# RWKV-7 recurrence stage: one step for both head pairs of a group, row-tiled image products, decay applied after the add, masks read from PSUM

## The chip, the cores and the metric

The kernel runs on one core of a Trainium2 chip. The metric is device time in microseconds (us) of one execution of the whole program. TensorE (PE) multiplies into PSUM, VectorE (DVE) and ScalarE (ACT) work element by element and can read PSUM, GpSimd (POOL) works element by element on SBUF alone, and SyncE (SP) issues most DMA transfers. Each engine runs its instructions in a fixed order and waits on semaphores for the others.

## The reference, cut to what matters

The program is two layers of a hybrid backbone over 1024 latent and 256 context tokens: an attention and RG-LRU layer, a mixture of experts, an RWKV-7 time-mixing layer, and a second mixture of experts. The change touches the RWKV-7 recurrence alone, which runs in both directions for 16 heads of 64 x 64 state:

```python
def wkv_scan(s0, decay, k, v, kk, a, r, reverse):
    ...
    def step(s, inp):
        w_t, k_t, v_t, a_t, b_t = inp[:5]
        sa = jnp.einsum('bhvk,bhk->bhv', s, a_t)
        s = s * w_t[:, :, None, :] + sa[..., None] * b_t[:, :, None, :] + v_t[..., None] * k_t[:, :, None, :]
        y = jnp.einsum('bhvk,bhk->bhv', s, inp[5]) if r is not None else None
        return s, y
    s_fin, ys = lax.scan(step, s0, xs, reverse=reverse)
    ...
```

It runs over the context first and then, from that state, over the latent tokens.

## The kernel before, in words

Class `Wkv` (lines 1880 to 2196) computes the recurrence in chunks of C = 64 tokens. There are 20 chunks (4 of context, 16 latent) for each of 4 head groups (`pg`), and so 80 group-chunks. A group holds two head pairs (`i`) in two directions (`d`): four units `u`, each with two heads `h` on the two halves of the partitions. Groups 0 and 1 go through all chunks together, then groups 2 and 3. Eight group-chunks (two groups, four chunks) make a batch, so there are ten batches.

- `prep` (L1937) handles two chunks of one group. It loads the key images `bk` and the query images `ar` by DMA. The product `G` (L1977) gives, for each unit, all products of the two within a chunk. In `ar` the two heads lie side by side with zeros in the other half (the memsets L1964 and L1965), so that one 128-row product serves both heads. ACT copies the solve's part of `G` into `lab` (L1981, L1982) and the output part into `lrb` (L1984); DVE multiplies the part for `ar` by a triangular mask (L1987) and POOL masks `lrb` in place (L1990). POOL scales the key images by the chunk's total decay `gC` into `bs` (L1956); PE transposes `bs` (L1996) and ACT copies it out as `bkt` (L1997). `G` has one buffer of two PSUM banks.
- `solve` (L2020) inverts the triangular matrices of one batch, all 32 units at once. It transposes `lab` into `lp` (L2028), runs 62 dependent DVE instructions of 31 to 256 elements (L2036, L2037), and transposes the result back (L2039 into `lp`, and four quarter transposes L2043 into `dtb`).
- `join` (L2046) completes the inverse: PE (L2055, which reads `lp`), ACT (L2058), PE (L2062), ACT (L2064). `lp`, `rp` and `tmp` have one buffer each, so the next solve can't start before the join has read `lp`.
- `values` (L2001) transposes the values into `sv`.
- `step` (L2066) advances one pair `i` of one group by one chunk. Its PE products are X (L2077), U (L2082), the first part of Y (L2087), S (L2093) and the second part of Y (L2101), with `xs` (L2079) and `sv` (L2089) copied by ACT between them. DVE adds the decayed state `pg` to S (L2116), ACT copies the sum into the next chunk's `sv` (L2120), and POOL multiplies the sum by `gC` for the step after (L2125). ACT copies Y out (L2129).

`run` (L2138) emits the work: `prep` up to 17 group-chunks ahead (as many buffers as `ar`, `lrb` and `bkt` have), `solve` and `join` of a batch just ahead of its steps. The order on each engine is then chosen by the framework's scheduler, from a simulated timeline with the emission order as priority, and is fixed in the program. In what follows a position is one group-chunk going through `step`.

After the recurrence, `mix_out1` multiplies the outputs by the output matrix and prepares the second mixture of experts; its pieces are named `tail` and are partly woven into the last steps.

Of the kernel before, what the change touches and what calls it, by code (L numbers as in the profile page):

```python
# [1879 lines left out]
class Wkv:  # L1880
# [20 lines left out]
    def __init__(self, g, p, pp):  # L1901
# [35 lines left out]
    def prep(self, b):  # L1937
# [16 lines left out]

        bs = self.bs.rearrange("p (c u x) -> p c u x", c=2, u=4)
        nc.gpsimd.tensor_tensor(bs, bk, g.gC[:, c0:c0 + 2, 4 * pg:4 * pg + 4, None].to_broadcast([128, 2, 4, 2 * C]), op=ALU.mult)  # L1956
        for k in range(2):
# [6 lines left out]
            nc.gpsimd.memset(ar[64:128, :, 0:w], 0.0)  # L1964
            nc.gpsimd.memset(ar[0:64, :, 2 * C:2 * C + w], 0.0)  # L1965
# [100 lines left out]
    def step(self, b, gr, i, nxt, ys, dense=False):  # L2066

        g, nc, p, pp = self.g, self.g.nc, self.p, self.pp
        ar, lrb, bkt, sv, c, dtb = gr["ar"], gr["lrb"], gr["bkt"], gr["sv"], gr["c"], b["dtb"]
# [3 lines left out]
        us = slice(2 * i, 2 * i + 2)
        X, U, S, Y = (ps[:, k] for k in range(4))
        for h, d in HD:
            u = 2 * i + d
            nc.tensor.matmul(X[R[h], C * d:C * d + C], ar[:, u, 2 * C * h:2 * C * h + C], sv[:, u, C * h:C * h + C], start=True, stop=True)  # L2077
        xs = p.tile([128, 2, C], F, name="xs", tag="xs", bufs=self.XB)
        nc.scalar.copy(xs, X.rearrange("p (d v) -> p d v", d=2))  # L2079
        for d in range(2):  # L2080
# [293 lines left out]
```

## Time and profile before

| quantity | value |
|---|---|
| median of 3 runs | 3741.8 us (3740.38 to 3742.62) |
| profiled execution | 3742.38 us, of which the span 3740.6 us |
| first image product to last output of the recurrence | 2220 us to 3012 us |
| the ten solves on DVE | first starts at 2239.9 us, last at 2839.7 us |
| mean granted clock of TensorE | 0.93 |
| busy share of the span | PE 88%, DVE 73%, ACT 62%, POOL 28% |

The profile is of one execution, taken by the hardware profiler. PE's busy time is that of its records, whose ends are modelled and include the time in which a result drains; a float32 matmul leaves two records. "Idle before" in a group of instructions is how long the engine stood still ahead of them, and the name behind the arrow is what ended that.

### The profile page before, as it was taken

The numbers are of one execution on the slowest core, as the hardware profiler recorded it, in microseconds if no ns is written. First come the engines' busy times: TensorE is split into PE (matmuls) and PEld (weight loads), VectorE is DVE, ScalarE is ACT, GpSimd is POOL, SyncE is SP. The second block draws the span as 40 slices with busy tenths as digits, with TensorE's granted clock in tenths as the row PEclk, the third lists the DMA queues.
The fourth block names the chain that finished last, engine by engine and source line by source line (L and its number), as shares of the span: only waits on it lengthen the run. The fifth ranks groups of instructions, "written<-read, shape, count | busy, mean of one in ns | idle before, by whom it ended". The sixth has DMA issues, their size and how long they took to land. (4 is left out here: it accounts for less than half of the span.)

```text
span 3740.6 us, 65805 instructions
## 1 busy us (share of the span) xinstructions
PE 3296.5 (88%) x25097; PEld 2565.2 (69%) x25097; DVE 2724.6 (73%) x3869; ACT 2312.7 (62%) x4629; POOL 1048.8 (28%) x1045
## 2 busy tenths in 40 slices
PE   7997989599999999697798867899897885999998
PEld 5884677477777777577776855677676564887776
DVE  5666773667666666667976987778678557888888
ACT  4564573366666666335644654788787554778776
POOL 2213002211111111235734663444344222111111
PEclk9998999799999999898898986999898897999999
DMA  5217715478888887335753773333335569999995
GB/s 199 64 31 278 271 56 182 158 265 283 294 286 281 280 296 275 112 116 159 223 148 92 213 193 80 88 92 96 85 92 156 162 207 330 380 379 385 354 381 217
DMA packets 579363, 770.45 MB, mean 206 GB/s; under 512 B 106868, under 2 KB 371048, under 8 KB 572904
## 3 DMA queue, kind: packets, MB, share of 16 engines
q1 hardware_dynamic: 564104, 717.22, 57.6%
q0 software_dynamic: 14944, 49.03, 4.8%
q8 instruction: 198, 3.24, 0.4%
q14 instruction: 117, 0.96, 0.1%
HBM read 638.96 MB, written 127.18 MB: 205 GB/s over the span
## 5 line engine op out<-in xcount | busy, mean ns | idle before, releaser
L192 DVE TENSOR_TENSOR elo<-raw,ehi 128x2048 fp32r<-128x2048 f32 x378 | 859.6, 2289 | 296.0 <-ACT ehi L191 294.8
L191 ACT ACTIVATE ehi<-raw 128x2048 fp32r<-128x2048 f32 x384 | 734.8, 1917 | 212.1 <-PE h L1158 82.6
L1158 PE MATMUL h<-ehi,xhi 128*128 128x512 f32 x512 | 208.0, 406 | 0.0
L1158 PE MATMUL h<-elo,xhi 128*128 128x512 f32 x512 | 202.9, 396 | 0.0
L1158 PE MATMUL h<-ehi,xlo 128*128 128x512 f32 x512 | 202.8, 396 | 0.0
L1102 PE MATMUL h<-ehi,wx 128*128 128x512 f32 x512 | 163.3, 396 | 0.0
L1477 PE MATMUL pj<-mvh,whi 128*128 128x384 f32 (+1 forms) x512 | 149.8, 326 | 2.9 <-ACT vv L1787 2.9
L1477 PE MATMUL pj<-mvl,whi 128*128 128x256 f32 (+1 forms) x512 | 147.3, 322 | 3.8 <-POOL mvl L192 2.9
L1477 PE MATMUL pj<-mvh,wlo 128*128 128x256 f32 (+1 forms) x512 | 149.1, 323 | 0.9 <-POOL wlo L192 0.7
L2037 DVE TENSOR_TENSOR rp<-rp,tmp 128x31 f32<-128x31 f32 (+15 forms) x310 | 141.8, 457 | 8.2
L1977 PE MATMUL G<-ar,early 128*128 128x256 f32 (+1 forms) x440 | 127.2, 443 | 22.2 <-issue 9.9
L1265 PE MATMUL y<-ehi,wh 128*128 128x512 f32 x512 | 143.6, 397 | 1.9 <-DVE wh L192 1.9
L1122 POOL DMA_INDIRECT xg<-s_hl,idx x16 | 15.8, 985 | 451.2 <-PE tr L1137 446.8
L2036 DVE TENSOR_TENSOR tmp<-lp,rp 128x31 f32<-128x31 f32 (+15 forms) x310 | 127.4, 411 | 8.1
L1080 ACT ACTIVATE xm<-tr,c_mcol 128x128 f32<-128x128 f32 x256 | 95.3, 452 | 60.9 <-PE tr L1069 35.9
L2120 ACT COPY sv<-st 64x128 f32<-64x128 f32 x304 | 89.9, 296 | 59.7 <-DVE st L2116 54.8
L1087 POOL DMA_INDIRECT xg<-s_hl,idx x16 | 24.1, 1509 | 361.4 <-PE tr L1069 339.1
L191 ACT ACTIVATE whi<-wraw 128x1024 fp32r<-128x1024 f32 x62 | 65.5, 1057 | 88.3 <-PE pj L1477 54.9
L1977 PEld LDWEIGHTS G<-ar,early 128*128 128x128 f32 x440 | 91.6, 232 | 41.0 <-issue 17.8
L216 PE MATMUL pj<-xhi,whi 128*128 128x512 f32 (+1 forms) x336 | 119.1, 355 | 0.0
L216 PE MATMUL pj<-xlo,whi 128*128 128x512 f32 (+1 forms) x336 | 119.0, 354 | 0.0
L216 PE MATMUL pj<-xhi,wlo 128*128 128x512 f32 (+1 forms) x336 | 118.8, 354 | 0.0
(565 smaller groups left out, 9772.7 us busy)
## 6 DMA issues: line engine op xcount, KB each, us to landing
raw<-in_exp_w SPq DMA_DIRECT2D x379, 1024.0 KB
modw<-in_mod_w SPq DMA_DIRECT2D x48, 1024.0 KB
wraw<-in_rw_rkv SPq DMA_DIRECT2D x48, 512.0 KB
s_iAR<-ar SPq DMA_DIRECT2D x32, 384.0 KB
s_iBK<-bk SPq DMA_DIRECT2D x32, 384.0 KB
ar<-s_iAR SPq DMA_DIRECT2D x88, 128.0 KB
early<-s_iBK SPq DMA_DIRECT2D x40, 256.0 KB
early<-s_iBK SPq DMA_DIRECT2D x80, 128.0 KB
```

What stands on the lines that cost most here:

```text
L191: nc.scalar.activation(hi, src, AF.Copy)
L192: (sub or nc.vector).tensor_tensor(lo, src, hi.bitcast(F), op=ALU.subtract)
L216: nc.tensor.matmul(ps[:m, :b - a], wt[:, k, :m], xt[:, k, a:b], start=k == 0 and n == 0, stop=k == kt - 1 and n == 2)
L1080: self.nc.scalar.activation(f[:, k], src[:, k], AF.Identity, scale=a, bias=b)
L1102: nc.tensor.matmul(hs[which], a[:, kk], b[:, k], start=kk == 0 and a is x[0] and b is w[1], stop=kk == 7 and a is x[1])
L1158: nc.tensor.matmul(hs[which], a[:, kk], b[:, k], start=kk == 0 and a is x[0] and b is w[1], stop=kk == 7 and a is x[1])
L1265: nc.tensor.matmul(y[:, 512 * n:512 * n + 512], a[:, kk % 4], b[:, k, 512 * n:512 * n + 512], start=kk == 0 and a is hh and b is hi, stop= ...
L1477: nc.tensor.matmul(ps[q], wk[:, k], xk[:, a:b], start=k == 0 and n == 0, stop=k == KT - 1 and n == 2)
L1977: nc.tensor.matmul(gp[:, u, :, 0:w], bk[:, k, u], ar[:, u].rearrange("p (h x) -> p h x", h=2)[:, :, 0:w], start=True, stop=True)
L2036: nc.vector.tensor_tensor(t, lp[:, k + 1:, k:k + 1].to_broadcast([128, n, w]), rp[:, k:k + 1, 0:w].to_broadcast([128, n, w]), op=ALU.mult)
L2037: nc.vector.tensor_tensor(rp[:, k + 1:, 0:w], rp[:, k + 1:, 0:w], t, op=ALU.subtract)
L2120: nc.scalar.copy(nxt(R[h], C * h), st[R[h]])
```

## The change

- `step` takes both pairs of a group at once. Each of its five products has eight matmuls of the four units in a row (heads alternating), each ACT copy and DVE instruction is of twice the width, and there is half their number. X and U lie in one PSUM bank, S and Y in a second; `XS` has two buffers of two banks where it had four of one. The first part of Y is emitted ahead of U.
- The product `G` is split by heads: each unit has two matmuls over 64 rows (row tiles at partitions 0 and 64) that write to two different banks, in place of one over 128 rows with zeros. The memsets of `ar` go.
- The decay is applied to the sum: DVE adds the old state to S and then multiplies the sum by `gC`. POOL's scaling of `bk` into `bs` and POOL's product `pg` go; the transposes read `bk`.
- DVE writes the masked `lrb` straight from PSUM; ACT's copies and POOL's mask of `lrb` go.
- In `solve`, one transposition over all partitions and two ACT copies take the place of four quarter transpositions into `dtb`.

```diff
-    NX = 4
+    NX = 2
...
-        bs = self.bs.rearrange("p (c u x) -> p c u x", c=2, u=4)
-        nc.gpsimd.tensor_tensor(bs, bk, g.gC[:, c0:c0 + 2, 4 * pg:4 * pg + 4, None].to_broadcast([128, 2, 4, 2 * C]), op=ALU.mult)
...
-            nc.gpsimd.memset(ar[64:128, :, 0:w], 0.0)
-            nc.gpsimd.memset(ar[0:64, :, 2 * C:2 * C + w], 0.0)
...
-            gp = pp.tile([128, 4, 2, gw], F, name="G", tag=gt, bufs=bufs)
+            gp = pp.tile([128, 2, 4, 2 * C], F, name="G", tag=gt, bufs=bufs)
...
-                nc.tensor.matmul(gp[:, u, :, 0:w], bk[:, k, u], ar[:, u].rearrange("p (h x) -> p h x", h=2)[:, :, 0:w], start=True, stop=True)
+                for h, own, oth, cc in HH:
+                    nc.tensor.matmul(gp[:, h, u, 0:w], bk[own, k, u], ar[own, u, cc:cc + w], start=True, stop=True)
...
-                if not ctxt:
-                    nc.scalar.copy(lrb[own], gp[own, :, h, C:])
...
-                nc.vector.tensor_tensor(o4, g4, self.mask[oth, None, :, 0:w].to_broadcast([64, 2, 2, w]), op=ALU.mult)
-            if not ctxt:
-                lb = lrb.rearrange("p (i d) t -> p i d t", d=2)
-                nc.gpsimd.tensor_tensor(lb, lb, self.mask[:, None, :, C:].to_broadcast([128, 2, 2, C]), op=ALU.mult)
+                parts = [(ar[oth, :, cc:cc + w], oth, slice(0, w))] + ([] if ctxt else [(lrb[own], own, slice(C, 2 * C))])
+                for out, r, x in parts:
+                    o4, g4 = (t.rearrange("p (i d) t -> p i d t", d=2) for t in (out, gp[r, h, :, x]))
+                    nc.vector.tensor_tensor(o4, g4, self.mask[r, None, :, x].to_broadcast([64, 2, 2, x.stop - x.start]), op=ALU.mult)
...
-                nc.tensor.transpose(tp[:, u], bs[:, k, u], g.ident)
+                nc.tensor.transpose(tp[:, u], bk[:, k, u], g.ident)
...
-        for q in range(4):
-            r = slice(32 * q, 32 * q + 32)
-            o = 32 * (q % 2)
-            nc.vector.transpose(dtb[r, :, o:o + 32].rearrange("p u t -> p t u"), rp[r])
+        nc.vector.transpose(dtb[:, :, 32:].rearrange("p u t -> p t u"), rp)
+        for h in range(2):
+            a = slice(64 * h, 64 * h + 32)
+            nc.scalar.copy(dtb[a, :, 0:32], dtb[a, :, 32:])
...
+        for h, u in HU:
+            nc.tensor.matmul(X[R[h], u], ar[:, u, 2 * C * h:2 * C * h + C], sv[:, u, V[h]], start=True, stop=True)
+        xs = p.tile([128, 4, C], F, name="xs", tag="xs", bufs=self.XB)
+        nc.scalar.copy(xs, X)
...
+            st = p.tile([128, 4, C], F, name="st", tag="st", bufs=3)
+            if c:
+                nc.vector.tensor_tensor(st, S, self.st.pop(pg), op=ALU.add)
+            gc = g.gC[:, c, 4 * pg:4 * pg + 4, None]
+            nc.vector.tensor_tensor(st, st if c else S, gc.to_broadcast([128, 4, C]), op=ALU.mult)
             for h in range(2):
+                nc.scalar.copy(nxt[R[h], :, V[h]], st[R[h]])
+            self.st[pg] = st
```

Line numbers shift by the lines removed: L1969 is the new G product, L1979 the new masks, L2017 and L2029 the first and last transposition of a solve, L2025 and L2026 its 62 instructions, L2086 the add and L2088 the product by `gC`, and on ACT L1973 and L1974 `lab`, L1986 `bkt`, L2003 and L2004 `sv` from `values`, L2067 `xs`, L2075 `sv` from U, L2090 the next `sv`, L2095 Y.

On DVE, from the end of the fifth solve to the start of the sixth (a batch of context chunks), the order before is:

```order
L2043 STREAM_TRANSPOSE dtb_19741<-rp 32x32x32 x4
L2116 TENSOR_TENSOR st<-XS,pg 128x128
L1987 TENSOR_TENSOR ar<-G,wmask 64x4x64 x2
L2116 TENSOR_TENSOR st<-XS,pg 128x128 x3
L1987 TENSOR_TENSOR ar<-G,wmask 64x4x64 x2
L2028 STREAM_TRANSPOSE lp<-lab 128x1024
```

The changed kernel has there, as the first twelve of its rows:

```order
L2029 STREAM_TRANSPOSE dtb_19741<-rp 128x32x32
L1979 TENSOR_TENSOR ar<-G,wmask 64x4x64 x2
L2086 TENSOR_TENSOR st<-XS,st 128x256
L2088 TENSOR_TENSOR st<-st,gC 128x256
L1979 TENSOR_TENSOR ar<-G,wmask 64x4x64 x2
L2086 TENSOR_TENSOR st<-XS,st 128x256
L2088 TENSOR_TENSOR st<-st,gC 128x256
L2086 TENSOR_TENSOR st<-XS,st 128x256
L2088 TENSOR_TENSOR st<-st,gC 128x256
L1979 TENSOR_TENSOR ar<-G,wmask 64x4x64 x4
L2086 TENSOR_TENSOR st<-XS,st 128x256
L2088 TENSOR_TENSOR st<-st,gC 128x256
```

Between two solves there stood the masks of two group-chunks and the adds of two positions; now there stand the masks of six group-chunks and the adds of six positions, and correspondingly fewer inside the solves. Over the solves 2 to 9 the counts inside a solve go from 94 `ar` masks and 92 adds of one pair to 42 `ar` masks, 38 `lrb` masks and 42 instructions of the new add and product; after a solve they go from 34 `ar` masks to 86 (5.4 group-chunks a gap).

On ACT, in steady state, a position with the copies of a `G` stands before as (two pairs' copies, `values`, and the first half of a `G`):

```order
L2120 COPY sv<-st 64x2x64 x2
L2129 COPY ys<-XS 128x2x64
L2014 COPY sv<-T 64x4x64
L2015 COPY sv<-T 64x4x64
L2120 COPY sv<-st 64x2x64 x2
L2129 COPY ys<-XS 128x2x64
L2120 COPY sv<-st 64x2x64 x2
L2129 COPY ys<-XS 128x2x64
L1981 COPY lab<-G 32x256
L1982 COPY lab<-G 32x4x32
L1984 COPY lrb<-G 64x256
```

and in the changed kernel as

```order
L2075 COPY sv<-XS 64x4x64 x2
L1986 COPY bkt<-T 128x512
L2067 COPY xs<-XS 128x256
L2003 COPY sv<-T 64x4x64
L2004 COPY sv<-T 64x4x64
L2095 COPY ys<-XS 128x2x128
L2090 COPY sv<-st 64x4x64 x2
L1973 COPY lab<-G 32x256
L1974 COPY lab<-G 32x4x32
```

One copy over both pairs stands where two narrower ones stood, and no `lrb` copy follows those of `lab`.

## Rows read from the trace of the kernel before

**Rows 1.** Busy time of each engine in a window, whole recurrence: window, length, engines, clock, DMA.
```profile
2310.00:3012.00 702.00, 615.49 (x9230) 471.94 (x9230) 523.81 (x1033) 524.07 (x1826) 282.26 (x408) 0.91 0.43 114
```
**Rows 2.** Instructions of line 2028, the first transposition of each solve.
```profile
L2028 DVE STREAM_TRANSPOSE lp<-lab x10: 1911/1956/1978, 2239.9 to 2839.7; 128x1024 f32<-128x1024 f32 x10
```
**Rows 3.** Windows: the seven solves from 2379.8 us, the first and the sum.
```profile
2379.80:2433.20 53.40, 49.38 (x738) 39.04 (x734) 47.11 (x91) 42.82 (x139) 24.59 (x36) 0.97 0.44 104
...
sum 368.10, PE 327.30 PEld 262.62 DVE 331.38 ACT 298.33 POOL 164.41; mean PE 46.76 PEld 37.52 DVE 47.34 ACT 42.62 POOL 23.49
```
**Rows 4.** Windows: the seven gaps behind those solves, the sum.
```profile
sum 91.80, PE 83.38 PEld 68.03 DVE 27.21 ACT 70.77 POOL 28.76; mean PE 11.91 PEld 9.72 DVE 3.89 ACT 10.11 POOL 4.11
```
**Rows 5.** DVE by lines, 2379.8 to 2839.7 us: busy, mean ns, idle before, releasers.
```profile
L2037 DVE TENSOR_TENSOR rp<-rp,tmp 128x31 f32<-128x31 f32 (+15 forms) x217 | 99.8, 460 | 5.9
L2036 DVE TENSOR_TENSOR tmp<-lp,rp 128x31 f32<-128x31 f32 (+15 forms) x217 | 87.0, 401 | 5.6
L2043 DVE STREAM_TRANSPOSE dtb<-rp 32x1024 f32<-32x1024 f32 x28 | 53.7, 1919 | 0.3
L1987 DVE TENSOR_TENSOR ar<-G,wmask 64x512 f32<-64x512 f32 (+1 forms) x82 | 52.2, 637 | 27.3 <-ACT lrb L1984 19.6 <-ACT lab L1982 6.3
L2116 DVE TENSOR_TENSOR st<-XS,pg 128x128 f32<-128x128 f32 x104 | 28.5, 283 | 17.0 <-PE XS L2101 8.7 <-ACT sv L2120 3.0 <-PE XS L2093 2.5
L1987 DVE TENSOR_TENSOR early<-G,wmask 64x512 f32<-64x512 f32 x30 | 20.7, 688 | 24.6 <-ACT lrb L1984 24.1
L2039 DVE STREAM_TRANSPOSE lp<-rp 128x1024 f32<-128x1024 f32 x7 | 14.7, 2105 | 0.2
L2028 DVE STREAM_TRANSPOSE lp<-lab 128x1024 f32<-128x1024 f32 x7 | 13.7, 1957 | 23.8 <-ACT lab L1982 23.8
```
**Rows 6.** Timeline of DVE and POOL: start, length, engine, line, tiles.
```profile
2644.88 0.19 DVE L2036 TENSOR_TENSOR tmp<-lp,rp 128x31 f32<-128x31 f32 x1
...
2648.74 1.90 POOL L1956 TENSOR_TENSOR early<-early,gC 128x1024 f32<-128x1024 f32 x1
2648.81 2.00 DVE L2036 TENSOR_TENSOR tmp<-lp,rp 128x156 f32<-128x156 f32 x1
...
2667.74 0.43 DVE L2036 TENSOR_TENSOR tmp<-lp,rp 128x256 f32<-128x256 f32 x1
```
**Rows 7.** ACT by lines and shapes, 2379.8 to 2839.7 us.
```profile
L2120 ACT COPY sv<-st 64x128 f32<-64x128 f32 x213 | 63.1, 296 | 38.5 <-DVE st L2116 34.9
L2089 ACT COPY sv<-XS 64x128 f32<-64x128 f32 x224 | 58.2, 260 | 5.1 <-PE XS L2087 1.7 <-PE XS L2082 0.3
...
L1984 ACT COPY lrb<-G 64x256 f32<-64x256 f32 x97 | 35.5, 366 | 1.2
L1997 ACT COPY bkt<-T 128x512 f32<-128x512 f32 x56 | 32.9, 588 | 1.8 <-PE XS L2093 0.9
...
L2079 ACT COPY xs<-XS 128x128 f32<-128x128 f32 x110 | 26.3, 271 | 1.4
L2129 ACT COPY ys<-XS 128x128 f32<-128x128 f32 x94 | 25.0, 265 | 1.8
```
**Rows 8.** Timeline of PE: products of a step (x8 is four matmuls) and of G.
```profile
2496.57 0.46 PE L2093 MATMUL XS<-sv,bkt 128*64 128x64 f32 x8
...
2496.96 0.45 PE L2101 MATMUL XS<-sv,lrb 64*64 64x64 f32 x8
...
2507.77 1.20 PE L2077 MATMUL XS<-sv,ar 128*64 128x64 f32 x32
...
2508.95 1.97 PE L1977 MATMUL G<-ar,early 128*128 128x256 f32 x8
```
**Rows 9.** Line 1987 by shapes, 2219 to 3012 us: its narrow form.
```profile
L1987 DVE TENSOR_TENSOR ar<-G,wmask 64x256 f32<-64x256 f32 x22 | 9.3, 422 | 8.0 <-ACT lab L1982 6.3 <-issue 1.3
```
**Rows 10.** Timeline of DVE: start of the second solve, end of the last.
```profile
2309.30 1.95 DVE L2028 STREAM_TRANSPOSE lp<-lab 128x1024 f32<-128x1024 f32 x1 [5.04 <-ACT lab L1982]
...
2898.53 7.68 DVE L2043 STREAM_TRANSPOSE dtb<-rp 32x1024 f32<-32x1024 f32 x4
```

More of the change, by code (lines that the diff above doesn't have):

```diff
@@ L2064, in join, with step @@
                 nc.scalar.copy(dtb[a, u0:u0 + 16, 32:], tp[a])
-    def step(self, b, gr, i, nxt, ys, dense=False):
+    def step(self, b, gr, nxt, ys):
         g, nc, p, pp = self.g, self.g.nc, self.p, self.pp
-        ar, lrb, bkt, sv, c, dtb = gr["ar"], gr["lrb"], gr["bkt"], gr["sv"], gr["c"], b["dtb"]
-        ps = pp.tile([128, 4, 2 * C], F, name="XS", tag="XS", bufs=self.NX)
-        HD = [(h, d) for h in range(2) for d in range(2)]
+        ar, lrb, bkt, sv, pg, c, dtb = gr["ar"], gr["lrb"], gr["bkt"], gr["sv"], gr["pg"], gr["c"], b["dtb"]
+        ps = pp.tile([128, 2, 2, 4, C], F, name="XS", tag="XS", bufs=self.NX)
+        HU = [(h, u) for u in range(4) for h in range(2)]
@@ L2072, in step @@
         R = [slice(0, 64), slice(64, 128)]
[L2073 to L2080, printed above, removed]
-            for h in range(2):
-                nc.tensor.matmul(U[R[h], C * d:C * d + C], dtb[R[h], gr["lu"] + 2 * i + d], xs[R[h], d], start=True, stop=True)
@@ new lines, in step @@
+        V = [slice(C * h, C * h + C) for h in range(2)]
+        X, U, S, Y = ps[:, 0, 0], ps[:, 0, 1], ps[:, 1, 0], ps[:, 1, 1]
+        for h, u in HU:
+            nc.tensor.matmul(X[R[h], u], ar[:, u, 2 * C * h:2 * C * h + C], sv[:, u, V[h]], start=True, stop=True)
+        xs = p.tile([128, 4, C], F, name="xs", tag="xs", bufs=self.XB)
+        nc.scalar.copy(xs, X)
+        if ys is not None:
+            for h, u in HU:
+                nc.tensor.matmul(Y[R[h], u], ar[:, u, 2 * C * h + C:2 * C * h + 2 * C], sv[:, u, V[h]], start=u == 0, stop=False)
@@ new lines, in step @@
+        for h, u in HU:
+            nc.tensor.matmul(U[R[h], u], dtb[R[h], gr["lu"] + u], xs[R[h], u], start=True, stop=True)
+        for h in range(2):
+            nc.scalar.copy(sv[R[h], :, V[h]], U[R[h]])
+        if nxt is not None:
+            for h, u in HU:
+                nc.tensor.matmul(S[R[h], u], bkt[:, u, V[h]], sv[:, u, V[h]], start=ys is None, stop=ys is None)
+        if ys is not None:
+            for h, u in HU:
+                nc.tensor.matmul(Y[R[h], u], lrb[R[h], u], sv[R[h], u, V[h]], start=False, stop=u == 3)
@@ L2128, in step @@
             to = (slice(0, 4, 3), slice(2, 0, -1))[c % 2]
-            nc.scalar.copy(ys[:, to, i], Y.rearrange("p (d v) -> p d v", d=2))
+            nc.scalar.copy(ys[:, to], Y.rearrange("p (i d) v -> p d i v", d=2))
     def finish(self, pg, ys, n):
@@ L2190, in run @@
                 to = [x for bb in (b, bs.get(k + 1)) if bb for x in bb["gr"] if (x["pg"], x["c"]) == (pg, c + 1)][0]["sv"]
-            for i in range(2):
-                us = slice(2 * i, 2 * i + 2)
-                self.step(b, gr, i, to and (lambda r, o, us=us: to[r, us, o:o + C]), ys[pg] if c >= 4 else None, at >= self.DENSE)
+            self.step(b, gr, to, ys[pg] if c >= 4 else None)
             if c >= 4 and c % 2:
@@ L2255, in __init__ @@
         T = [pp.tile([128, 512], F, name="T", tag="T", bufs=w.NT) for _ in range(w.NT)]
-        X = [pp.tile([128, 512], F, name="XS", tag="XS", bufs=w.NX) for _ in range(w.NX)]
+        X = [pp.tile([128, 2, 512], F, name="XS", tag="XS", bufs=w.NX) for _ in range(w.NX)]
+        X = [t[:, k] for t in X for k in range(2)]
         self.n = {"y": 0, "b": 0}
```

55 lines of the change are left out of this document (6 added, 49 removed).

## The prediction

> **What bounds the kernel now.** I read the windows of the whole stage first. From the first step to the last output it takes 702 us, with PE busy for 615, ACT and DVE for 524 each and POOL for 282 [rows 1]. No engine is full, so the pattern of the stage counts. The instructions of the solve's first transposition show it: there are ten, the first at 2239.9 us and the last at 2839.7 us [rows 2], and the second at 2309.3 [rows 10]. From the second to the tenth that is 530.4 us, a cycle of 66.3 us for each batch of eight positions.
>
> Seven cycles cut into the solve itself (368.1 us, 52.6 each) and the gap behind it (91.8 us, 13.1 each) tell two different stories. Inside a solve DVE works 331.4 of 368.1 us [rows 3]; with the small pauses between 62 dependent instructions it is full, and the solve lasts as long as the sum of what DVE has in its order there. In a gap DVE works only 27.2 of 91.8 us, while PE is busy for 83.4 and ACT for 70.8 [rows 4]: there steps, join and the last products `G` of the next batch go through PE and ACT, and the next solve waits for `lab` from ACT (23.8 us of idle time on the row of L2028 [rows 5]). So a cycle is DVE's sum in the solve plus the rate of PE and ACT in the gap. Over both, PE has 410.7 us of 459.9 for 56 positions, 7.3 us each, and ACT 369.1, 6.6 each. The gap holds the adds of two positions and the masks of 2.1 group-chunks on average; 2.1 positions at 6.6 us are 13.8, which agrees with 13.1.
>
> **The solve's own instructions.** The 434 instructions of L2036 and L2037 took 186.8 us in seven solves, 26.7 each [rows 5]. Some were held up: one of 156 elements took 2.00 us beside a POOL product of 1.90 us that started just before it, where clean ones take 0.19 us at 31 elements and 0.43 at 256 [rows 6]. A line through those two (0.157 us plus 1.07 ns per element) over the 62 instructions, with 2 x 5456 elements (31 x 1 + 30 x 2 + ... + 1 x 31, twice), gives 21.4 us, so 5.3 us of each solve are such stalls. The change leaves POOL nothing but a few memsets there, so I take all of them away; the bounds are none and all.
>
> The Trainium skill (SBUF — State Buffer, Who interferes with whom) says that a VectorE instruction with two SBUF inputs fully blocks against a GpSimd instruction that reads SBUF, and one that only writes doesn't matter; by that rule the remaining memsets cost nothing and the new product by `gC` meets nobody. That changes the lower bound of this term only: none left would be right.
>
> The four quarter transpositions took 53.7 us for seven solves, 7.7 each; one over all partitions should take what L2039 takes, 2.1 us. With the other two (13.7 and 14.7 over seven, 4.1 each solve) the solve's own work falls from 38.4 us to 21.4 + 4.1 + 2.1 = 27.6, and the pauses of 11.5 us over seven stay, 1.6 each [rows 5].
>
> **What else DVE has inside a solve.** The new order puts 42 `ar` masks, 38 `lrb` masks and 42 adds or products into eight solves. An `ar` mask takes 0.69 us [rows 5], an `lrb` mask of half the width 0.42 [rows 9]. An add from PSUM over 256 columns doesn't exist before; it lies between 0.28 (the 128-column one [rows 5]) and 0.56 (twice that), and the 256-element instruction from SBUF at 0.43 and the 256-column mask from PSUM at 0.42 are nearest, so I take 0.42, for the product too. Together (29.0 + 16.0 + 17.6) / 8 = 7.8 us. The solve becomes 27.6 + 1.6 + 7.8 = 37.0 us, 15.6 less than now. That much is gained inside the solve, and the gap has to take what was moved out.
>
> **The gap.** It now holds the masks of 5.4 group-chunks, and so some five positions with their `G`. On ACT the step's copies are 172.6 us of the seven cycles; at double width the same work takes 0.403 us for the copy from SBUF (0.296 plus 0.107 for 128 more columns, the difference of 0.366 and 0.260) and 0.37 for those from PSUM, half as many, 121.9 us in all. The `lrb` copies (35.5) go, and 14 new copies in the solve come, about 1.0 us each by extending 0.588 at 512 columns [rows 7]. ACT falls to 297.5 us, 5.3 a position. On PE a group of four matmuls starts 0.39 us before the next; sixteen in a row take 1.20 us where four take 0.46, so a matmul costs 0.062 and the change of product 0.14. Ten groups of four become five of eight: 3.9 to 3.2 us. If the row tiles of `G` run two at a time, its 1.97 us halve [rows 8]. PE falls from 7.3 to about 5.7 us a position. DVE has 86 `ar` masks, 74 `lrb` masks and 78 adds or products in eight gaps, 15 us each. POOL's waits are off all of these paths and go at no price.
>
> At PE's or ACT's rate 5.4 positions take 29 to 31 us. Against that stands that PE and ACT have only some three positions to do in the 37 us of the solve and can run ahead there: the first adds and masks of the gap are ready when it opens. The copies that ACT's order holds between the end of a solve and the last `lab` copy of the next batch come to 22 us on average, at these durations, the floor. I take 25.5, in the middle; bounds 22 and 31. The cycle is then 62.5 us against 66.3, 3.8 less, over eight cycles 30 us. DVE's whole sum is 37 + 15 = 52 us, so it is at 84% and the next thing late.
>
> The Trainium skill (TensorEngine Tiling (Array Packing), PSUM Bottleneck) warns that tiling speeds up TensorE and not the evacuation of PSUM. No run shows it here yet. `G` keeps its one buffer, so by that rule the halved `G` would bring nothing in the gap, and the time would be that of the row tile rival below.
>
> **Ends of the stage.** The first cycle lasts 69.4 us (2239.9 to 2309.3). There solve and masks sum to 27.6 + 1.6 + 12 x 1.11 = 42.5 and the waits for `G` of the first batches remain, 10 us less (6 to 15). The last solve runs from 2839.7 to 2906.2 us [rows 2, 10] with pieces of the tail between; its own work falls by 10.8 us, and I take 9 (5 to 12). The eight steps behind it run among the tail's large matmuls, which don't change: 0 (10 faster to 5 slower). From 3012 us on nothing is touched; the second mixture of experts just starts earlier.
>
> **The sum.** 30 + 10 + 9 = 49 us off the profiled 3742.4 (which is 0.6 above the median of the runs): 3693 us. With a gap of 22 and the better ends: 7.3 x 8 + 15 + 12 + 10 = 95, 3647 us. With 31 and the worse ends: a cycle of 68, 14 lost, 11 won, 5 lost, 3750 us.
>
> **The rivals.**
> - *ACT and PE set the whole gap.* No running ahead: 29 us, a cycle of 66, nothing won in the cycles; the ends keep 19 us: 3723 us. For it speaks that the gap of before follows the rate so closely.
> - *The row tiles of G don't overlap.* What the trace shows to overlap are tiles in different columns (pairs of 64-column tiles in a step), never two row tiles over the same columns. Then 8 half-row matmuls take as long as `G` now, PE needs 6.6 us a position, the gap becomes 25.5 + 5.4 x 0.9 = 30.4 and the cycle 67.4: 9 lost in the cycles, 19 won, 3732 us.
> - *Recurrence latency (slower).* A position's add, product, two wide copies and the next X are now one chain, with two chains under way instead of four, and one more DVE instruction between S and `sv`, queued behind the solve. Its pieces sum to five products at 0.46, 0.37 of `xs`, two copies at 0.37, add and product 0.84, two copies at 0.40, some 4.5 us without queues, and two chains share a round. It decides once a round (two positions) is over 66.3 / 4 = 16.6 us. At 18 us the cycle is 72: 46 lost, 10 won, 3778 us. Against it: before, positions passed in steady state at 8.2 us each and DVE, the queue in question, lets an add through after one or two solve instructions.
> - *More is won.* Steps run ahead inside the solve as far as buffers go, and the gap is at its floor: 3647 us.
>
> **Chances.** Forecast 0.45, more won 0.15, gap at the rate 0.15, row tiles in series 0.12, latency 0.13. The range of 3640 to 3750 leaves out the latency case and little else. Faster by over 0.2% (7.5 us, about what a measurement of this kernel can tell from no change), under 3734: the forecast, the gain, the rate case and half of the row tile case, less what of the forecast lies beyond, 0.76; within 0.2% 0.11; slower 0.13.
>
> **What would show it.** The first transposition L2017 of the second to tenth solve should be 62 us apart (now 66.3), from L2017 to the end of L2029 37 us; the solve's instructions should sum to about 21.4 us with none near 2 us; the new add and product at 0.42 each; a `G` of 16 records at about 1.1 us, else the row tiles run in series. Wrong would be: solves of 45 us or more (DVE waits inside for late steps), gaps of over 31 us, or L2090 waiting for L2088 by tens of us in total beyond the 34.9 us for L2116 now.

## The result and the profile after

The changed kernel takes 3757.6 us (median of five runs, 3753.0 to 3766.7) against 3740.4 us (3728.0 to 3742.6) for the kernel before: a ratio of 1.0056, 95% interval 1.0033 to 1.0078. It is slower by 0.6%; the forecast was 3693 us, in a range of 3640 to 3750. The profiled execution, the longest of the five, took 3766.7 us, of which the span is 3764.9, 24.3 more than before.

Busy time in the recurrence, as in [rows 1] (window, length, PE, PEld, DVE, ACT, POOL, granted clock, DMA share, GB/s); the last Y copy starts at 3032.0 us where it started at 3012.0:

```profile
2310.00:3030.00 720.00, 576.89 (x9662) 458.07 (x9659) 485.70 (x1079) 434.69 (x1258) 54.49 (x49) 0.84 0.41 110
```

Every engine works less than in [rows 1] (PE 577 against 615, ACT 435 against 524, POOL 54 against 282), and the stage still takes longer. The first transposition of the solves, as in [rows 2]:

```profile
L2017 DVE STREAM_TRANSPOSE lp<-lab x10: 1924/1931/1949, 2243.0 to 2859.2; 128x1024 f32<-128x1024 f32 x10
```

The second starts at 2293.4, so eight cycles take 565.8 us, 70.7 each, where they took 66.3. Windows of the seven solves from 2360.1 us, and of the seven gaps behind them, the sums, as in [rows 3, 4]:

```profile
sum 254.80, PE 199.35 PEld 164.13 DVE 235.42 ACT 134.06 POOL 0.00; mean PE 28.48 PEld 23.45 DVE 33.63 ACT 19.15 POOL 0.00
...
sum 244.30, PE 193.13 PEld 166.62 DVE 109.08 ACT 173.78 POOL 16.97; mean PE 27.59 PEld 23.80 DVE 15.58 ACT 24.83 POOL 2.42
```

A solve lasts 36.4 us (before 52.6) and a gap 34.9 (before 13.1). Inside a solve PE now works 28.5 and ACT 19.2 of 36.4 us; before they worked 46.8 and 42.6 of 52.6. The new idle time of ACT and PE lies beside the solve. DVE by lines from 2360.1 to 2859.2 us, as in [rows 5]:

```profile
L2026 DVE TENSOR_TENSOR rp<-rp,tmp 128x31 f32<-128x31 f32 (+15 forms) x217 | 74.3, 343 | 6.8
L2025 DVE TENSOR_TENSOR tmp<-lp,rp 128x31 f32<-128x31 f32 (+15 forms) x217 | 74.2, 342 | 7.1
L1979 DVE TENSOR_TENSOR ar<-G,wmask 64x512 f32<-64x512 f32 (+1 forms) x82 | 51.8, 632 | 67.5 <-ACT lab L1974 58.5 <-PE T L1985 4.8 <-DMA ar<-s_iAR 3.5
L1979 DVE TENSOR_TENSOR lrb<-G,wmask 64x256 f32<-64x256 f32 x96 | 40.5, 422 | 1.6
L2088 DVE TENSOR_TENSOR st<-st,gC 128x256 f32<-128x256 f32 x52 | 23.0, 442 | 1.1
L2086 DVE TENSOR_TENSOR st<-XS,st 128x256 f32<-128x256 f32 x52 | 21.9, 422 | 21.5 <-PE XS L2081 18.5 <-ACT bkt L1986 1.5 <-PE XS L2078 0.5
L1979 DVE TENSOR_TENSOR early<-G,wmask 64x512 f32<-64x512 f32 x30 | 20.5, 683 | 43.5 <-ACT lab L1974 43.5
```

DVE now waits for ACT: 58.5 and 43.5 us ahead of its two groups of `ar` masks. ACT by lines in the same stretch, as in [rows 7], waits in its turn:

```profile
L2090 ACT COPY sv<-st 64x256 f32<-64x256 f32 x108 | 43.6, 403 | 14.6 <-DVE st L2088 12.0
...
L2095 ACT COPY ys<-XS 128x256 f32<-128x256 f32 x48 | 17.9, 372 | 59.2 <-DVE st L2086 58.8
```

The span's 24.3 us, from the starts and ends of the solves: the first solve starts 3.1 later, the first cycle is 19.0 shorter (50.4 against 69.4), eight cycles are 35.4 longer, the last solve is 12.3 shorter, its end to the last Y copy 12.8 longer (118.6 against 105.8), and the rest 4.3 longer.

### The profile page after: what moved, and what is told of

Its sections match the earlier page's. It is cut to its first block, busy times and chain, and to the rows that moved or that the text cites. A ratio compares the mean times of both kernels' runs of the same rounds, so it can differ in the third digit from the quotient of the medians.

```text
span 3764.9 us, 65798 instructions
## 1 busy us (share of the span) xinstructions
PE 3264.1 (87%) x25737; PEld 2560.1 (68%) x25737; DVE 2685.2 (71%) x3963; ACT 2228.6 (59%) x4065; POOL 783.8 (21%) x637
## 5 line engine op out<-in xcount | busy, mean ns | idle before, releaser
L1969 PE MATMUL G<-ar,early 64*128 64x128 f32 (+1 forms) x880 | 98.6, 361 | 76.2 <-DVE lrb L1979 50.4
L1969 PEld LDWEIGHTS G<-ar,early 64*128 64x128 f32 x880 | 83.1, 255 | 85.3 <-issue 44.2
L2019 POOL MEMSET rp<- 128x1024 f32 x10 | 9.5, 952 | 589.8 <-DVE dtb L2029 587.5
L1979 DVE TENSOR_TENSOR ar<-G,wmask 64x512 f32<-64x512 f32 (+1 forms) x110 | 69.4, 631 | 82.3 <-ACT lab L1974 73.0
L1165 PE MATMUL hc<-raw,xc 128*32 128x256 f32 x2048 | 117.1, 381 | 0.0
L191 ACT ACTIVATE whi<-wraw 128x1024 fp32r<-128x1024 f32 x62 | 65.5, 1056 | 84.4 <-PE pj L1477 51.7
L2025 DVE TENSOR_TENSOR tmp<-lp,rp 128x31 f32<-128x31 f32 (+15 forms) x310 | 108.0, 349 | 9.9
L2026 DVE TENSOR_TENSOR rp<-rp,tmp 128x31 f32<-128x31 f32 (+15 forms) x310 | 107.0, 345 | 9.5
```

Of the source, the lines that this page charges most:

```text
L191: nc.scalar.activation(hi, src, AF.Copy)
L1165: nc.tensor.matmul(hc[32 * q:32 * q + 32, :256], xcs[e][:, kk], raws[kk // 4, q // 2][:, kk % 4, 256 * (q % 2):256 * (q % 2) + 256], start ...
L1969: nc.tensor.matmul(gp[:, h, u, 0:w], bk[own, k, u], ar[own, u, cc:cc + w], start=True, stop=True)
L2025: nc.vector.tensor_tensor(t, lp[:, k + 1:, k:k + 1].to_broadcast([128, n, w]), rp[:, k:k + 1, 0:w].to_broadcast([128, n, w]), op=ALU.mult)
L2026: nc.vector.tensor_tensor(rp[:, k + 1:, 0:w], rp[:, k + 1:, 0:w], t, op=ALU.subtract)
```

## The experiments

Four theories were tested. Theory 1: the one buffer of `G` makes product, `lab` copies and masks a chain. Theory 2: the recurrence's latency sets the gap. The clock theory: with the row tiles of `G` the granted clock falls, and all products get slower. The order theory: the scheduler deals the row-tiled `G` another order on each engine, and that order costs. In the table, cycle is the mean from the second to the tenth solve's start, solve and gap the means of the eight in it, and clock is the granted clock there. The column "adds" counts the positions whose add stands inside a solve in DVE's order, a mean of eight; the first chunk of a group has no add and is left out (84 adds of one pair in the eight solves before, where the 92 above hold eight copies too). The kernel before took 3739.1 to 3740.9 us in these comparisons.

| kernel | us | ratio, 95% interval | cycle | solve | gap | clock | adds |
|---|---|---|---|---|---|---|---|
| before | 3740.4 | 1 | 66.3 | 53.2 | 13.1 | 0.92 | 5.25 |
| after | 3757.6 | 1.0056 (1.0033–1.0078) | 70.7 | 36.7 | 34.0 | 0.82 | 2.25 |
| g_split | 3765.8 | 1.006 (1.004–1.0079) | 72.9 | 42.9 | 30.0 | 0.77 | 3.5 |
| pairs_apart | 3765.5 | 1.006 (1.004–1.008) | 73.5 | 39.6 | 33.9 | 0.76 | 3.4 |
| lrb_undone | 3777.9 | 1.0093 (1.0076–1.011) | 73.1 | 35.3 | 37.8 | 0.79 | 2.25 |
| decay_undone | 3768.9 | 1.0076 (1.0053–1.0098) | 70.1 | 40.9 | 29.1 | 0.83 | 2.75 |
| g_rows_alone | 3818.2 | 1.021 (1.019–1.023) | 79.0 | 42.7 | 36.2 | 0.78 | 2.3 |
| g_wide | 3704.5 | 0.9898 (0.9881–0.9914) | 63.7 | 46.5 | 17.3 | 0.92 | 5.25 |
| g_twice | 3836.0 | 1.025 (1.0231–1.027) | 77.1 | 34.6 | 42.5 | 0.84 | 1.75 |
| g_wide8 | 3697.9 | 0.9888 (0.9872–0.9905) | 62.7 | 46.0 | 16.6 | 0.93 | 5.25 |
| rows_order_wide | 3683.4 | 0.9846 (0.9826–0.9865) | 60.9 | 45.3 | 15.6 | 0.87 | 5.25 |
| wide8_order_rows | 3809.8 | 1.0189 (1.0172–1.0206) | 73.8 | 37.6 | 36.2 | 0.88 | 2.25 |
| rows_dve_order | 3732.0 | 0.9984 (0.9974–0.9995) | 67.7 | 50.7 | 17.0 | 0.82 | 5.25 |
| rows_pe_act_order | 3749.7 | 1.0025 (1.0016–1.0035) | 70.0 | 37.0 | 33.0 | 0.79 | 2.6 |
| solve_alone | 3765.8 | 1.0071 (1.0054–1.0088) | 68.6 | 42.5 | 26.1 | 0.91 | 4.1 |
| solve_order_before | 3757.4 | 1.0037 (1.002–1.0055) | 67.2 | 48.2 | 18.9 | 0.90 | 5.2 |

### The two first theories of the gap

**g_split** gives each head of `G` a tile of its own:

```diff
-            gp = pp.tile([128, 2, 4, 2 * C], F, name="G", tag=gt, bufs=bufs)
...
+                gp = [pp.tile([128, 4, 2 * C], F, name=f"G{h}", tag=f"G{h}", bufs=1) for h in range(2)]
...
```

> The changed kernel with G as two PSUM tiles of one bank, one for each head, in place of one tile of two banks; nothing else. Theory 1 (the one G tile is a chain: product 1.16 us, lab copies 1.25, masks 2.25, and waits, one group-chunk every 5.8 us in the gaps): the two heads overlap, a group-chunk needs 4 us or less, the gap falls from 34.0 to about 26 us, the cycle from 70.7 to about 63, the time from 3757.6 to about 3695 us (3680 to 3720). Theory 2 (the latency of the recurrence, two chains instead of four, sets the gap): the gap stays at 32 to 35 us and the time at 3745 to 3760 us. That the scheduler only bunches masks behind solves, whatever G does, would leave the masks' waiting for lab as it is and the time at 3745 to 3765 us.

**pairs_apart** takes the step back to one pair at a time:

```diff
...
-            self.step(b, gr, to, ys[pg] if c >= 4 else None)
+            for i in range(2):
+                self.step(b, gr, i, to, ys[pg] if c >= 4 else None)
```

> The changed kernel with one step for each pair again (XS four tiles of one bank, copies and DVE instructions of half the width and twice the number); row tiles of G, masks out of PSUM, decay on the sum and the new transpositions stay. Theory 2 (latency of the recurrence with two chains): the gap falls from 34.0 to 26 us or less, 3757.6 to about 3695 us. Theory 1 (G's chain): the gap stays at its 5.8 us for each group-chunk; ACT and DVE get about 1.3 and 0.6 us a position more, so 3757 to 3790 us.

**lrb_undone** copies `lrb` by ACT and masks it on POOL, as before:

```diff
+                if not ctxt:
+                    nc.scalar.copy(lrb[own], gp[own, h, :, C:])
...
+                nc.gpsimd.tensor_tensor(lb, lb, self.mask[:, None, :, C:].to_broadcast([128, 2, 2, C]), op=ALU.mult)
```

> The changed kernel with lrb copied by ACT from PSUM and masked by POOL in place, as before; all else as changed. Theory 1 (G's chain of lab, masks): two copies of 0.37 us come into the chain and two masks of 0.42 us leave it, a group-chunk stays at 5.6 to 5.8 us, the gap at 32 to 35 us and the time at 3745 to 3765 us. If the masks' time on DVE itself is what costs (DVE's sum), 0.84 us x 8 = 6.7 us leave each cycle: about 3704 us.

**decay_undone** puts the decay back on POOL:

```diff
+        nc.gpsimd.tensor_tensor(bs, bk, g.gC[:, c0:c0 + 2, 4 * pg:4 * pg + 4, None].to_broadcast([128, 2, 4, 2 * C]), op=ALU.mult)
...
-            nc.vector.tensor_tensor(st, st if c else S, gc.to_broadcast([128, 4, C]), op=ALU.mult)
...
+                nc.gpsimd.tensor_tensor(st, st, gc.to_broadcast([128, 4, C]), op=ALU.mult)
```

> The changed kernel with the decay as before: POOL scales bk into bs, and POOL multiplies the state by gC behind the copies, off the chain from S to the next X; POOL's products and their stalls of DVE come back. In the traces so far a position takes 8.3 us before and 8.8 after, inside a solve and behind it alike, whatever the solve's length, so the steps' own chain and not DVE's sum in the solve is the bound. If that is so and the product of 0.44 us in the chain counts: solves 3 to 5 us longer, gaps shorter by more, the cycle 70.7 to 68 to 69 us, 3735 to 3750 us. If DVE's sum counted: solves and cycle 3 to 5 us longer, 3780 to 3800 us.

None of the four is faster than the changed kernel, and neither theory got the gap it asked for: with four chains it is 33.9 us, with `G` in two tiles 30.0, and there the solve grew by 6.2. The times of g_split (by 1 us), lrb_undone and decay_undone lie outside every range given for them; that of pairs_apart lies in theory 1's. The table also shows why such edits tell little by themselves: each made the scheduler deal another order (2.25 to 3.5 adds in a solve). What speaks against both theories as main causes comes further down: rows_order_wide keeps the one buffer and the two chains, and its gap is 15.6 us.

One reading holds beside that: with the POOL products of decay_undone, an instruction of the solve takes 0.40 to 0.42 us on average, and in the changed kernel 0.34. Its two lines in decay_undone, and one in g_wide, where POOL has memsets alone:

```profile
L2028 DVE TENSOR_TENSOR rp<-rp,tmp 128x112 f32<-128x112 f32 (+15 forms) x245 | 102.5, 418 | 8.0
L2027 DVE TENSOR_TENSOR tmp<-lp,rp 128x135 f32<-128x135 f32 (+15 forms) x245 | 97.7, 399 | 7.8
...
L2026 DVE TENSOR_TENSOR tmp<-lp,rp 128x31 f32<-128x31 f32 (+15 forms) x279 | 97.9, 351 | 7.9
```

### The row tiles of G

**g_rows_alone** puts the row tiles alone into the kernel before, without the memsets:

```diff
...
-                nc.tensor.matmul(gp[:, u, :, 0:w], bk[:, k, u], ar[:, u].rearrange("p (h x) -> p h x", h=2)[:, :, 0:w], start=True, stop=True)
+                for h, own, oth, cc in HH:
+                    nc.tensor.matmul(gp[h][:, u, 0:w], bk[own, k, u], ar[own, u, cc:cc + w], start=True, stop=True)
```

> The kernel before with the row tiles of G alone (two matmuls over 64 rows for each unit in two banks, no memsets of ar). In the four kernels with row tiles so far the granted clock over the recurrence was 0.75 to 0.82 and the cycle 70.7 to 73.5 us; in the two without it was 0.90 and 0.91 and 66.3 and 68.6 us. Clock theory (halving G's work on TensorE lowers the granted clock, and all products of a step get slower): clock at or below 0.85, a cycle of 69 us or more, 3755 to 3780 us although G itself is shorter. Rival (row tiles cost nothing, other parts of the change slow it): clock 0.88 or more, G's 0.6 to 0.9 us a position won in part, 3715 to 3742 us.

**g_wide** does the converse in the changed kernel, with the memsets back:

```diff
-                for h, own, oth, cc in HH:
-                    nc.tensor.matmul(gp[:, h, u, 0:w], bk[own, k, u], ar[own, u, cc:cc + w], start=True, stop=True)
+                nc.tensor.matmul(gp[:, u, :, 0:w], bk[:, k, u], ar[:, u].rearrange("p (h x) -> p h x", h=2)[:, :, 0:w], start=True, stop=True)
```

> The changed kernel with G as one 128-row product for both heads again, with the memsets of ar on POOL; all else as changed. Clock theory: the granted clock over the recurrence goes from 0.82 to about 0.9, the cycle from 70.7 to 66 us or less and the time from 3757.6 to 3700 to 3735 us, although PE does more. Rival: G's 0.8 us more for each position in its chain lengthens the gap, 3765 to 3790 us.

**g_twice** issues each of the row-tiled matmuls a second time:

```diff
+                for h, own, oth, cc in HH:
+                    nc.tensor.matmul(gp[:, h, u, 0:w], bk[own, k, u], ar[own, u, cc:cc + w], start=True, stop=True)
```

> The changed kernel with every matmul of G issued twice, the second over the same PSUM addresses, so that TensorE does more work and the result is the same. Clock theory: the clock rises to 0.86 to 0.92 and the time falls or stays, 3715 to 3757 us. Rival: 0.5 to 1.0 us more in G for each position, 4 to 8 us a cycle, 3775 to 3815 us.

The row tiles alone cost the kernel before 2.1%, and without them the rest of the change gains 1.0%. The times of g_rows_alone and g_twice lie above both ranges given for them, that of g_wide in the clock theory's. Of the 71 us by which the profiled g_rows_alone is longer, 24 lie behind the last Y copy, where 31 of the 128 records of the tail's large matmuls (L853) then stand and before none. Windows over the eight cycles, of before, of g_rows_alone, of the changed kernel and of g_wide, one fence each:

```profile
2309.30:2839.70 530.40, 468.54 (x7468) 375.93 (x7469) 410.04 (x800) 422.92 (x1353) 224.14 (x351) 0.92 0.38 94
```
```profile
2295.00:2926.80 631.80, 506.08 (x8106) 416.17 (x8106) 406.59 (x810) 432.13 (x1386) 169.25 (x230) 0.78 0.33 82
```
```profile
2293.40:2859.20 565.80, 445.88 (x8065) 376.07 (x8066) 394.60 (x891) 353.81 (x902) 18.07 (x21) 0.82 0.35 89
```
```profile
2299.70:2809.70 510.00, 434.20 (x7652) 355.31 (x7652) 390.20 (x890) 354.30 (x903) 80.07 (x148) 0.92 0.40 101
```

The clock falls with the row tiles, as the clock theory says. But g_twice has a higher clock than the changed kernel (0.84 against 0.82) and takes 78 us more. Beside the clock, the number of adds in a solve is lower too in every kernel so far that has row tiles (1.75 to 3.5, against 4.1 to 5.25 without). So the two had to be parted.

### The order, with the same instructions

**g_wide8** has eight matmuls of `G`, as with row tiles, but of 128 rows, and POOL's memsets:

```diff
-                    nc.tensor.matmul(gp[:, h, u, 0:w], bk[own, k, u], ar[own, u, cc:cc + w], start=True, stop=True)
+                    nc.tensor.matmul(gp[:, h, u, 0:w], bk[:, k, u], ar[:, u, cc:cc + w], start=True, stop=True)
```

> The changed kernel with G as eight 128-row matmuls of 128 columns (one for each unit and head, over the zeros of ar that POOL's memsets write): as many instructions as with row tiles, but whole columns of the array. The order on DVE then has 5.25 positions of adds inside a solve on average, as with one 128-row product (5.25), against 2.25 with row tiles. Order theory (the framework's simulated timeline puts row tiles late, and the order that follows is what costs) and clock theory (half rows lower TensorE's clock) both expect about 3705 us (3695 to 3725), a cycle near 64 us. If it were the number of matmuls of G, 3750 us or more.

**rows_order_wide** is the changed kernel with the orders on DVE, TensorE and ScalarE fixed by tables of places read from g_wide8 (an edge between neighbours on an engine, no semaphore); **wide8_order_rows** is g_wide8 with the changed kernel's table:

```diff
+    for a, b in zip(order, order[1:]):
+        tc.add_manual_dep(found[b], found[a].name, info, reason="order")
```

> The changed kernel, row tiles of G and all, with the order of the recurrence's instructions on DVE, TensorE and ScalarE fixed to that of the kernel with eight 128-row matmuls (edges of order alone, no semaphore added). Order theory: solves with over 6 positions, cycle at or below 64 us, 3680 to 3715 us. Clock theory: the granted clock stays at 0.85 or below, and the time at 3735 to 3765 us.

> The converse: G as eight 128-row matmuls, with the order on DVE, TensorE and ScalarE fixed to that of the changed kernel (row tiles). Order theory: four positions inside a solve and four behind it, cycle 70 us or more, 3755 to 3790 us. Clock theory: clock 0.88 or more, cycle 64 to 67 us, 3700 to 3730 us.

Windows over the eight cycles of rows_order_wide, with the sums of its solves and of its gaps, and behind them the sum of the eight solves of the changed kernel; then the windows of g_wide8 and of wide8_order_rows over the cycles:

```profile
2296.50:2783.60 487.10, 413.23 (x8046) 351.02 (x8048) 386.87 (x887) 353.13 (x902) 14.46 (x19) 0.87 0.41 103
...
sum 362.50, PE 309.94 PEld 259.64 DVE 326.24 ACT 256.48 POOL 0.00; mean PE 38.74 PEld 32.45 DVE 40.78 ACT 32.06 POOL 0.00
...
sum 124.60, PE 103.29 PEld 91.38 DVE 60.63 ACT 96.65 POOL 14.46; mean PE 12.91 PEld 11.42 DVE 7.58 ACT 12.08 POOL 1.81
...
sum 293.50, PE 230.96 PEld 190.22 DVE 270.63 ACT 160.04 POOL 0.00; mean PE 28.87 PEld 23.78 DVE 33.83 ACT 20.00 POOL 0.00
```
```profile
2298.40:2799.70 501.30, 444.10 (x8162) 388.79 (x8162) 386.90 (x886) 353.12 (x901) 76.37 (x145) 0.93 0.40 101
```
```profile
2305.70:2896.20 590.50, 469.96 (x8064) 409.71 (x8064) 394.59 (x889) 353.94 (x900) 79.03 (x147) 0.88 0.35 87
```

The order theory holds both ways. With the other order the row-tiled kernel takes 3683.4 us, 74 less than with its own, 56 less than the kernel before (3739.1 in this comparison), and the fastest here. The 128-row one takes 112 more with the changed kernel's order, and with 3809.8 us lies above the order theory's range. At one order the row tiles themselves gain: 14.5 us (3697.9 to 3683.4) and 52 us (3809.8 to 3757.6). In these gains are the memsets that the 128-row kernels need; PE waits for them some 5 us in g_wide8 and 6 in wide8_order_rows between 2300 and 2860 us. The clock does not decide: rows_order_wide has 0.87 and is the fastest, wide8_order_rows 0.88. ACT's work over the eight cycles is 353 to 354 us in all four of these kernels, but in rows_order_wide 256 of it lies in the solves, against 160 in the changed kernel. The place of the adds tells the same. DVE's order from the end of the fifth solve to the start of the sixth in rows_order_wide, where the changed kernel has six positions' adds and six group-chunks' masks:

```
L2029 STREAM_TRANSPOSE dtb_19741<-rp 128x32x32
L1979 TENSOR_TENSOR ar<-G,wmask 64x4x64 x2
L2086 TENSOR_TENSOR st<-XS,st 128x256
L2088 TENSOR_TENSOR st<-st,gC 128x256
L1979 TENSOR_TENSOR ar<-G,wmask 64x4x64 x2
L2086 TENSOR_TENSOR st<-XS,st 128x256
L2088 TENSOR_TENSOR st<-st,gC 128x256
L1979 TENSOR_TENSOR ar<-G,wmask 64x4x64 x2
L2086 TENSOR_TENSOR st<-XS,st 128x256
L2088 TENSOR_TENSOR st<-st,gC 128x256
L2017 STREAM_TRANSPOSE lp<-lab 128x1024
```

**rows_dve_order** fixes DVE's order alone, **rows_pe_act_order** that of TensorE and ScalarE alone, with the same tables. The first, against rows_order_wide:

```diff
         pin(tc, [i for i in new if str(i.engine) == "EngineType.DVE"], ORDER_DVE)
-        pin(tc, [i for i in new if str(i.engine) == "EngineType.PE"], ORDER_PE)
-        pin(tc, [i for i in new if str(i.engine) == "EngineType.Activation"], ORDER_Activation)
```

> The changed kernel with only DVE's order of the recurrence fixed to that of the kernel with eight 128-row matmuls; TensorE's and ScalarE's are the scheduler's own. If the solve's place on DVE is what costs: 3675 to 3710 us and over 6 positions in a solve. If it is the rows of TensorE and ScalarE: 3735 us or more.

> The converse: TensorE's and ScalarE's order fixed, DVE's the scheduler's own, which again has only 2.6 positions of adds in a solve (2.25 in the changed kernel, 5.25 in the other order). If the solve's place on DVE is what costs: 3735 us or more, about four positions in a solve and four behind it. If it is the rows of TensorE and ScalarE: 3680 to 3710 us.

DVE's order alone wins 26 us, the other two alone 8, all three 74. The first expectation was missed on both sides: 3732.0 us, with 6.5 positions in a solve by the copies of `xs`, but solves of 50.7 us. The second came out as expected if DVE's order is what costs: 3749.7 us, four positions in a solve and four behind it. DVE's order is the larger part, and 40 of the 74 us come only with all three: the engines' orders have to fit each other.

### Is the solve the bound at all?

**solve_alone** is the kernel before with the new transposition:

```diff
-        for q in range(4):
-            r = slice(32 * q, 32 * q + 32)
-            o = 32 * (q % 2)
-            nc.vector.transpose(dtb[r, :, o:o + 32].rearrange("p u t -> p t u"), rp[r])
+        nc.vector.transpose(dtb[:, :, 32:].rearrange("p u t -> p t u"), rp)
+        for h in range(2):
+            a = slice(64 * h, 64 * h + 32)
+            nc.scalar.copy(dtb[a, :, 0:32], dtb[a, :, 32:])
```

> The kernel before with the new transposition of the solve alone (one over all partitions and two ACT copies in place of four quarter ones). If a shorter solve shortens the cycle as forecast (DVE full inside the solve), 5.6 us leave each of 8 cycles, the cycle goes from 66.3 to about 61 us and the time from 3740.4 to about 3690 us. If a shorter solve is given back in the gap, because then steps and G have less time beside the solve, the gap grows from 13.1 by 3 to 5 us and the time is 3725 to 3740 us.

**solve_order_before** is the same with the order of the kernel before.

> The kernel before with the new transposition of the solve alone, and with the order of the recurrence's instructions on DVE, TensorE and ScalarE fixed to that of the kernel before (the two new ScalarE copies stand ahead of the join's first). With the scheduler's own order the same edit took 3765.8 us, slower by 0.7%, with solves of 42.5 us and gaps of 26.1. Order theory (the forecast's sum holds as long as the order stays): 5.6 us leave each solve, the gap stays near 13 us, the cycle goes from 66.3 to 60 to 63 us, 3695 to 3715 us. Rival (the steps' own rate of 8.3 us a position is the bound in any order): the gap grows to 17 us or more, 3725 to 3742 us.

With the scheduler's own order, solve_alone has solves shorter by 10.7 us and gaps longer by 13.0, and 3765.8 us lies above both ranges given for it; its order is another one (4.1 adds in a solve). Sums of the eight solves and of the eight gaps, of the kernel before and then of solve_order_before:

```profile
sum 425.20, PE 372.64 PEld 297.81 DVE 379.01 ACT 342.90 POOL 192.09; mean PE 46.58 PEld 37.23 DVE 47.38 ACT 42.86 POOL 24.01
...
sum 105.20, PE 95.90 PEld 78.11 DVE 31.02 ACT 80.02 POOL 32.05; mean PE 11.99 PEld 9.76 DVE 3.88 ACT 10.00 POOL 4.01
...
sum 385.70, PE 351.89 PEld 280.32 DVE 334.00 ACT 322.12 POOL 173.82; mean PE 43.99 PEld 35.04 DVE 41.75 ACT 40.27 POOL 21.73
...
sum 151.50, PE 126.44 PEld 103.12 DVE 30.49 ACT 118.35 POOL 49.46; mean PE 15.81 PEld 12.89 DVE 3.81 ACT 14.79 POOL 6.18
```

In the same order, 4.9 us less in a solve come back as 5.8 us more in a gap. This was my own theory's expectation, and it failed. DVE does 5.7 us less in a cycle and stands still 6.6 us longer; what steps and products need on PE and ACT (59.8 and 55.1 of 67.2 us a cycle) does not get shorter. ACT has the two new copies on top, 2.1 us a cycle ahead of the join's first copy; how much of the 5.8 us is theirs was not parted.

That the whole kernel takes 0.4% more is another matter. Y copies and the tail's large matmuls of L853, the kernel before and then solve_order_before:

```profile
L2129 ACT COPY ys<-XS x128: 243/265/298, 2387.3 to 3012.0; 128x128 f32<-128x128 f32 x128
L853 PE MATMUL G<-early x32: 592/593/697, 2955.4 to 3010.6; 128*128 128x512 f32 x32
...
L2129 ACT COPY ys<-XS x128: 258/266/296, 2386.5 to 3010.3; 128x128 f32<-128x128 f32 x128
L853 PE MATMUL G<-early x32: 592/592/697, 2972.9 to 3026.1; 128*128 128x512 f32 x32
```

The last Y copy starts 1.7 us earlier than before. The profiled execution is 17.9 us longer, and all of that arises behind it, where 30 of the 128 records of L853 now stand (19.2 us) and before none; the fixed order covers the recurrence alone, and the tail stands later than before. So the time of 3757.4 us, above both ranges, decides nothing. The cycles do: the rival's gap of 17 us or more came (18.9).

## Why the prediction was wrong, step by step

- **What bounds the kernel: wrong.** "A cycle is DVE's sum in the solve plus the rate of PE and ACT in the gap" put a price on each microsecond of the solve. solve_order_before shows no such price in the kernel before: by it, eight times 5.6 us would have been won, and the last output came 1.7 us earlier. A full engine over a stretch was read as the bound, though the stretch behind it could take up what it released; the batch's eight steps need PE and ACT over solve and gap together.
- **The solve: right.** Forecast 37.0 us, measured 36.7; the 434 instructions took 148.5 us, 21.2 a solve (forecast 21.4). Add and product took 0.42 and 0.44 us, the `lrb` mask 0.42. The Trainium skill's rule (SBUF — State Buffer, Who interferes with whom) that a VectorE instruction with two SBUF inputs contends with a GpSimd instruction that reads SBUF, and not with one that only writes it, is borne out: with POOL's memsets beside it in g_wide, an instruction of the solve takes 0.34 to 0.35 us on average, as in the changed kernel without them, and with POOL's products in decay_undone 0.40 to 0.42.
- **The gap: the term that failed.** Forecast 25.5 us with bounds 22 and 31, measured 34.0. The sentence that PE and ACT "can run ahead" in the solve was against the row that the forecast itself used: with 2.25 adds in a solve, no more steps than that can be finished there, and ACT works 19.2 of 36.4 us there. A position took 9.2 us beside a solve and 8.5 behind it, where the forecast had 4.7 in the gap. These are means by the copies of `xs`, of which 32 of 64 stand in the eight solves. The order of DVE was read from the program and taken as a shift of work; it was the cost, as rows_order_wide shows: the same instructions in another order have a gap of 15.6 us and a cycle of 60.9. Of the three signs of being wrong this one came, a gap of over 31 us; solves of 45 us and L2090 waiting long for L2088 (12.0 us in all) did not.
- **Ends.** First cycle 19.0 us less (forecast 10), last solve 12.3 less (9); the steps behind it 12.8 more (0, at most 5): this bound was too narrow.
- **The rivals.** That ACT and PE set the rate fits solve_order_before; its time of 3723 us, with a gap of 29, took the order for given as well. Row tiles in series: no. `G` takes 1.16 us in 16 records at full clock (forecast 1.1). Latency: the sign came true and the round is 70.7 / 4 = 17.7 us against the 16.6 from which it decides, but not for the reason given; the same two chains turn round in 15.2 us in rows_order_wide, and four chains at 18.4 in pairs_apart. The pieces of its chain sum to 5.1 us and not to some 4.5; nothing else hangs on that sum.
- **The PSUM rule.** The Trainium skill (TensorEngine Tiling (Array Packing), PSUM Bottleneck) warns that tiling speeds up TensorE and not the evacuation of PSUM. The prediction took from it that the halved `G` would bring nothing, since its one buffer is emptied no faster. At one order the row tiles, with the memsets gone, brought 14.5 and 52 us; the measurement decides against that use of the warning here.
- **The sum in a fitting order.** rows_order_wide takes 3683.4 us and a cycle of 60.9 (forecast 3693 and 62.5). That they come so near the forecast is luck: its solve of 45.3 us is 8.3 longer than forecast, and its gap of 15.6 is 9.9 shorter. PE has 51.7 us of work in its cycle and ACT 44.1, where before they had 58.6 and 52.9; that this is where its 5.4 us come from is argued from these numbers, and shown only for `G` (g_wide8 to rows_order_wide: 3.9 us less on PE, 1.8 less a cycle).

Open is why the scheduler deals a row-tiled `G` another order than eight 128-row matmuls; its simulated timeline is in no trace.

## What to carry to other kernels

A stretch in which one engine is full is the bound only if the stretch behind it can't take up what is released: test it by shortening that engine's work at a fixed order. Where a scheduler sets the order, a change of the work also deals a new order, and this may be worth more than the work (74 and 112 us here, against 14.5 and 52 for the row tiles); compare kernels at one order before judging a part, and count in the new order what a long dependent run on one engine now shuts out. A fixed order taken from a sibling kernel can be kept: it gave the fastest version here.

## What the runs showed of the hardware

Two row tiles of 64 rows that write to different banks run at the same time, and their time follows the clock. Timeline of PE: two products `G` of 16 records in the changed kernel, and one of eight 128-row matmuls in g_wide8, also 16 records; then the windows around the first two, and that of the third (the clock is third from the end):

```profile
2466.78 2.08 PE L1969 MATMUL G<-early 64*128 64x128 f32 x16 [0.57 <-issue]
2472.48 1.16 PE L1969 MATMUL G<-early 64*128 64x128 f32 x16 [0.24 <-issue]
...
2453.32 2.05 PE L1971 MATMUL G<-early 128*128 128x128 f32 x16
```
```profile
2456.00:2466.70 10.70, 7.82 (x80) 6.31 (x80) 6.62 (x8) 6.27 (x14) 1.11 (x2) 0.66 0.23 65
...
2466.78:2468.86 2.08, 2.08 (x18) 1.85 (x20) 0.00 (x0) 0.00 (x0) 0.00 (x0) 0.50 0.10 37
2472.48:2473.64 1.16, 1.16 (x16) 0.97 (x16) 0.78 (x2) 0.69 (x2) 0.00 (x0) 1.00 0.90 194
...
2453.32:2455.37 2.05, 2.05 (x20) 1.93 (x20) 1.95 (x7) 1.54 (x5) 0.00 (x0) 1.00 0.10 28
```

At 2.4 GHz (granted 1.00) eight matmuls of 128 rows take 2.05 us and eight of 64 rows, with as many columns, 1.16. At 1.2 GHz (granted 0.50, after 10.7 us in which PE was busy for 7.8) the latter take 2.08. Over the eight cycles the granted clock lay between 0.76 and 0.88 in all kernels with row tiles or their order, and at 0.90 or above in the others; the fastest kernel is among the former.
